# Every fourth weight residue of the routed experts is computed on GpSimd instead of VectorE

## The chip, the core and the metric

The kernel runs on one core of a Trainium2 chip. The metric is the device time of one execution in microseconds (us): 2703.51 us is the median of three runs (2703.31 to 2705.68). The engines are called as in the profile: PE (matmuls; PEld is its loading of weights), ACT (ScalarE), DVE (VectorE), POOL (GpSimd) and SP, whose queue issues the loads.

## The reference, cut to what matters

The network is a stack of three blocks on 256 tokens of width 1024. Its last stage before the final norm is a mixture of 8 experts, each a gated MLP of inner width 3584, and the two best experts of each token count:

```
logits = (xt @ w_router).astype(jnp.float32)
top_v, top_i = lax.top_k(logits, TOP_K)          # TOP_K = 2 of 8 experts
gates = jax.nn.softmax(top_v, axis=-1)
comb = jnp.sum(jax.nn.one_hot(top_i, N_EXPERTS) * gates[..., None], axis=1)
for e in range(N_EXPERTS):
    y = y + comb[:, e:e+1] * swiglu(xt, wg[e], wu[e], wd[e])   # (silu(x@wg) * (x@wu)) @ wd
```

All of it is in 32-bit floats. The kernel computes a product of two such matrices from rounded parts: each operand is split into a high part (rounded to the type that the profile calls fp32r) and a low part, the rest, and the products high x high, high x low and low x high are added up.

## The kernel before, in words

The weights of the experts come as pieces of 128 x 2048 numbers (1 MB). An expert has 7 groups (`NG`), and a group needs 6 pieces: 2 of the gate matrix, 2 of the up matrix and 2 of the down matrix. So there are 8 x 7 = 56 groups and 336 pieces. Five experts have room for 128 tokens and are called big here; three have room for 64 and are called small (`CAPS`). In the order in which they run, they are big, big, small, big, big, small, big, small.

A piece goes through four steps. SP issues its load into one of 13 buffers (4 of `raw`, 6 of `raw2`, 3 of `raw3`; the profile calls all of them raw). Then `load_e` hands its two halves of 128 x 1024, called half-blocks here, to `conv_w` (line 465). There ACT writes the high part, whi (line 470), and DVE subtracts it from the raw half-block and writes the low part, wlo (line 471). There are 4 buffers of whi and 4 of wlo (`W_BUFS`), so the conversion of a half-block starts when PE is done with the one four places before it. PE then multiplies with both parts: in `up` the gate product eg and the up product eu, in `down` or `down_small` the sum eacc. A big expert has 6 matmuls of 512 columns for a half-block (two with whi, one with wlo, twice), a small one has 4.

Beside the subtractions, DVE has two other operations in each group: eal (line 486) and ea (2019) in a big expert, eas (2038) and eax (486) in a small one. ACT has the matching copies and activations, es (2014) and ea (2018) among them.

Each engine runs its instructions in the order of its own queue, and waits with all that stands behind when the one at the front waits. A scheduler writes these orders out when the program is built. POOL has 72 memsets of small borders in the stages before the experts (lines 833 and 1205) and four at the start, and nothing in the experts.

Of the kernel before, what the change touches and what calls it, by code (L numbers as in the profile page):

```python
# [251 lines left out]
def hybrid_stack_kernel(ctx: ExitStack, tc: tile.TileContext, A, out, voff, coff, stages=STAGES):  # L252
    nc = tc.nc
    pe, act, dve, pool = nc.tensor, nc.scalar, nc.vector, nc.gpsimd
# [11 lines left out]
    turns = {n: [0, [("work", c[0]), ("attn", c[1])]] for n, c in (("t1", N_T1), ("t2", N_T2))}  # L266
# [25 lines left out]
    def raw_tile():  # L292
        i = raws["n"] % sum(n for _, n in raws["slots"])
        raws["n"] += 1
        for name, n in raws["slots"]:
            if i < n:
                if name == "ring":
                    return ring.tile([P, 2048], F32, tag="raw", name="raw", bufs=RAW_BUFS)
                return pools[name].tile([P, 2048], F32, tag=name, name=name, bufs=n)
            i -= n  # L300
# [35 lines left out]
    def f32v(ap):  # L336
        return ap.bitcast(F32)
# [101 lines left out]
    def load(name, i):  # L439
        if (name, i) in ahead:  # L440
            return ahead.pop((name, i))
        raw = raw_tile()
        nc.sync.dma_start(raw, A[name][i])
        return [conv_w(raw[:, j * 1024 : (j + 1) * 1024]) for j in range(2)]

    def prefetch(name, i, half=None, steps=1, between=None):
        if half is not None:
            if not half:
                ahead[name, i] = []
                ahead["raw"] = ring.tile([P, 2048], F32, tag="raw", name="raw", bufs=RAW_BUFS)  # L450
            raw = ahead["raw"][:, half * 1024 : half * 1024 + 1024]
            for j in range(steps):
                cs = slice(j * 1024 // steps, (j + 1) * 1024 // steps)
                nc.sync.dma_start(raw[:, cs], A[name][i][:, half * 1024 + cs.start : half * 1024 + cs.stop])
                if between and not j:
                    between()
            ahead[name, i].append(conv_w(raw, steps))
        elif (name, i) not in ahead:
            ahead[name, i] = load(name, i)
# [2 lines left out]
        prefetch(name, 2 * w)  # L462
        prefetch(name, 2 * w + 1)

    def conv_w(raw, n=1):
        hi = ring.tile([P, 1024], F32R, tag="whi", name="whi", bufs=W_BUFS)
        lo = ring.tile([P, 1024], F32R, tag="wlo", name="wlo", bufs=W_BUFS)
        for i in range(n):
            cs = slice(i * 1024 // n, (i + 1) * 1024 // n)
            act.copy(hi[:, cs], raw[:, cs])  # L470
            dve.tensor_sub(lo[:, cs], raw[:, cs], f32v(hi[:, cs]))  # L471
        return hi, lo

    def load_last(name, i):

        raw = raw_tile()
        r = []
        for j in range(2):
            cs = slice(j * 1024, j * 1024 + 1024)
            nc.sync.dma_start(raw[:, cs], A[name][i][:, cs])  # L480
            r.append(conv_w(raw[:, cs], 1 + j))
        return r
# [1430 lines left out]
    def moe_round(rnd, hth, htl, sel0, sel, comb, rest=None):  # L1913
        regs = {}

        def fetch(raw, src, e, i, cs=slice(0, 2048)):
            if e not in regs:
                regs[e] = None
                if e:
                    regs[e] = nc.values_load(  # L1920
                        route["idx"][0:1, e : e + 1], engines=[mybir.EngineType.SP], min_val=0, max_val=NE - 1
                    )
            if e:
                w = A[src][bass.ds(regs[e], 1), i : i + 1, :, cs].rearrange("a b p n -> (a b p) n")
            else:
                w = A[src][0, i][:, cs]
            nc.sync.dma_start(raw[:, cs], w)

        def load_e(src, e, i):
            raw = raw_tile()  # L1930
            fetch(raw, src, e, i)
            return [conv_w(raw[:, j * 1024 : (j + 1) * 1024]) for j in range(2)]

        def load_e_last(src, e, i):

# [59 lines left out]
        def up(x, g, mid):  # L1995
            e, gx, big = x[0], x[1], x[4]
            po = [wv("eg"), wv("eu")]
            po = [a.rearrange("p a b -> p (a b)") for a in po]
            s = []
            for i, src in enumerate(("moe_g", "moe_u")):  # L2000
                if i and mid:
                    mid()
                for c in range(2):
                    wt = load_e(src, e, 2 * g + c)
                    for k4 in range(4):
                        k = 4 * c + k4
                        whi, wlo = wt[k4 // 2]
                        cs = slice((k4 % 2) * 512, (k4 % 2 + 1) * 512)
                        for a in gx:
                            mm(po[i], a[:, k, :], whi[:, cs], k == 0 and a is gx[0], False)  # L2010
                        mm(po[i], gx[0][:, k, :], wlo[:, cs], False, k == KD - 1)
                if not big:
                    s.append(t2("es", (P, 512)))
                    act.copy(s[i], po[i])
            if not big:
                return s
            a = t2("ea", (P, 512))
            act.activation(a, po[0], AF.Silu)
            dve.tensor_mul(a, a, po[1])
            return a  # L2020
# [22 lines left out]
        def down(x, g, a, acc):  # L2043
            e = x[0]
            ah, al = a
            for c in range(2):
                wt = load_e("moe_d", e, 2 * g + c)
                for j in range(2):
                    f = slice((2 * c + j) * P, (2 * c + j + 1) * P)
                    whi, wlo = wt[j]  # L2050
                    for n in range(2):
                        cs = slice(n * 512, (n + 1) * 512)
                        first = g == 0 and c == 0 and j == 0
                        mm(acc[n], ah[:, f], whi[:, cs], first, False)
                        mm(acc[n], al[:, f], whi[:, cs], False, False)
                        mm(acc[n], ah[:, f], wlo[:, cs], False, g == NG - 1 and c == 1 and j == 1)

        def down_small(x, g, a, acc):

            e = x[0]  # L2060
            for c in range(2):
                end = e == NE - 1 and g == NG - 1 and c == 1
                wt = (load_e_last if end else load_e)("moe_d", e, 2 * g + c)
                for j in range(2):
                    whi, wlo = wt[j]
                    for n in range(2):
                        cs = slice(n * 512, (n + 1) * 512)
                        mm(acc[n], a[:, 2 * c + j, :], whi[:, cs], g == 0 and c == 0 and j == 0, False)
                        mm(acc[n], a[:, 2 * c + j, :], wlo[:, cs], False, g == NG - 1 and c == 1 and j == 1)
# [130 lines left out]
```

## Time and profile before

| | us |
|---|---|
| median of three runs | 2703.51 |
| the profiled execution, its time | 2704.3 |
| its span, first to last instruction | 2702.4 |
| DVE busy | 2189.1 |
| PE busy | 2630.7 |
| ACT busy | 1733.5 |
| POOL busy | 7.7 |

Busy times of the engines lie beside each other, so they don't add up to the span. The experts take the stretch from about 1722 to 2686 us. A matmul's end is modelled in such a profile, so a PE that is shown as busy may wait a little; its waits are read from the weight loads (PEld).

### The profile page before, as it was taken

The page shows a single profiled execution, that of the slowest core. Times are in us where ns is not written, and L with a number is a line of the kernel's source. Part 1 is how long each engine was busy: PE and PEld are TensorE (multiplying, and loading weights), DVE is VectorE, ACT ScalarE, POOL GpSimd, SP SyncE. Part 2 cuts the span into 40 slices and gives each one's busy share as a digit, 9 for nine tenths or more (in the row PEclk, how much of TensorE's full clock was granted, in tenths as well). Part 3 has the DMA queues.
Part 4 walks back from the last instruction along what each step waited for, and adds up shares of the span by engine and source line. Part 5 has one row for each costly group of instructions (what it writes and reads, how often), then busy time and mean ns, then how long its engine had stood idle before and what let it go on. Part 6 is the DMA issues. An engine that isn't in the chain of part 4 may idle for free. (4 is left out here: it accounts for less than half of the span.)

```text
span 2702.4 us, 44795 instructions
## 1 busy us (share of the span) xinstructions
PE 2630.7 (97%) x17220; PEld 2319.6 (86%) x17220; DVE 2189.1 (81%) x3385; ACT 1733.5 (64%) x2605; POOL 7.7 (0%) x76
## 2 busy tenths in 40 slices
PE   8999999999989999999999999999999999999997
PEld 8789999998989988888999999888876778767875
DVE  8787587789768776667885569789999888999898
ACT  6665565565656555455654446577788777787787
POOL 0000000000000000000000000000000000000000
PEclk9999999999999999999999999999999999999999
DMA  7145345533535543343655555799999999999993
GB/s 265 63 158 200 134 153 192 179 110 107 175 109 184 188 145 125 126 156 102 250 189 188 187 178 184 259 340 355 364 373 393 351 347 340 359 408 369 341 377 154
DMA packets 87262, 620.07 MB, mean 229 GB/s; under 512 B 9936, under 2 KB 10064, under 8 KB 12800
## 3 DMA queue, kind: packets, MB, share of 16 engines
q1 hardware_dynamic: 86608, 616.57, 62.3%
q8 instruction: 137, 2.24, 0.3%
q14 instruction: 85, 0.70, 0.1%
q10 hardware_dynamic: 432, 0.56, 0.1%
HBM read 616.04 MB, written 1.05 MB: 228 GB/s over the span
## 5 line engine op out<-in xcount | busy, mean ns | idle before, releaser
L471 DVE TENSOR_TENSOR wlo<-raw,whi 128x1024 fp32r<-128x1024 f32 (+1 forms) x1164 | 1387.7, 1218 | 324.6 <-ACT whi L470 318.7
L470 ACT CAST whi<-raw 128x1024 fp32r<-128x1024 f32 (+1 forms) x1164 | 1189.8, 1048 | 550.7 <-PE wv L334 290.4
L334 PE MATMUL wv<-hh,whi 128*128 128x256 f32 x2400 | 679.2, 284 | 14.2 <-ACT hh L669 13.0
L334 PE MATMUL wv<-hl,whi 128*128 128x256 f32 x2400 | 678.2, 283 | 0.1
L334 PE MATMUL wv<-hh,wlo 128*128 128x256 f32 x2400 | 674.9, 283 | 2.1 <-DVE wlo L471 1.8
L334 PEld LDWEIGHTS wv<-hh,whi 128*128 128x128 f32 x2400 | 456.5, 191 | 17.6 <-ACT hh L669 13.8
L334 PEld LDWEIGHTS wv<-hh,wlo 128*128 128x128 f32 x2400 | 455.4, 190 | 4.6 <-DVE wlo L471 3.7
L334 PEld LDWEIGHTS wv<-hl,whi 128*128 128x128 f32 x2400 | 456.8, 190 | 1.9 <-DVE hl L670 0.7
L334 PE MATMUL eu<-whi,gx 128*128 128x512 f32 x728 | 245.7, 400 | 0.0
L334 PE MATMUL eg<-whi,gx 128*128 128x512 f32 x728 | 245.0, 398 | 0.0
L334 PE MATMUL eg<-wlo,gx 128*128 128x512 f32 x448 | 184.8, 412 | 10.2 <-DVE wlo L471 9.9
L334 PE MATMUL eu<-wlo,gx 128*128 128x512 f32 x448 | 185.0, 413 | 5.0 <-DVE wlo L471 4.2
L334 PEld LDWEIGHTS eg<-whi,gx 128*128 128x128 f32 x728 | 137.0, 190 | 29.6 <-ACT whi L470 0.6
L334 PE MATMUL acc<-fl,whi 128*128 128x256 f32 x576 | 161.6, 281 | 0.0
L334 PE MATMUL acc<-fh,whi 128*128 128x256 f32 x576 | 161.4, 281 | 0.1
L334 PE MATMUL acc<-fh,wlo 128*128 128x256 f32 x576 | 161.3, 280 | 0.0
L334 PEld LDWEIGHTS eu<-whi,gx 128*128 128x128 f32 x728 | 135.3, 188 | 27.2 <-ACT whi L470 0.9
L334 PEld LDWEIGHTS eg<-wlo,gx 128*128 128x128 f32 x448 | 84.5, 189 | 51.8 <-DVE wlo L471 34.5
L845 DVE SCALAR_TENSOR_TENSOR cv<-pad,vec,cv 128x256 f32<-128x256 f32 x288 | 124.7, 478 | 1.4 <-ACT cv L842 0.6
L334 PEld LDWEIGHTS eu<-wlo,gx 128*128 128x128 f32 x448 | 84.1, 188 | 40.2 <-DVE wlo L471 23.3
L334 PE MATMUL eacc<-whi,eah 128*128 128x512 f32 x280 | 110.5, 395 | 0.0
L334 PE MATMUL eacc<-whi,eal 128*128 128x512 f32 x280 | 110.5, 395 | 0.0
(564 smaller groups left out, 4177.9 us busy)
## 6 DMA issues: line engine op xcount, KB each, us to landing
raw<-moe_u SPq DMA_DIRECT2D x112, 1024.0 KB, 6.4
raw<-moe_g SPq DMA_DIRECT2D x112, 1024.0 KB, 6.5
raw<-moe_d SPq DMA_DIRECT2D x111, 1024.0 KB, 6.2
raw<-ffn_in SPq DMA_DIRECT2D x44, 1024.0 KB, 4.9
raw<-sw_in SPq DMA_DIRECT2D x28, 1024.0 KB, 4.9
raw<-ffn_out SPq DMA_DIRECT2D x22, 1024.0 KB, 4.9
raw<-hy_in SPq DMA_DIRECT2D x20, 1024.0 KB, 5.0
raw<-ssm_in SPq DMA_DIRECT2D x18, 1024.0 KB, 5.1
```

Of the source, the lines that this page charges most:

```text
L334: return pe.matmul(o, l, r, start=start, stop=stop, skip_group_check=True)
L470: act.copy(hi[:, cs], raw[:, cs])
L471: dve.tensor_sub(lo[:, cs], raw[:, cs], f32v(hi[:, cs]))
L845: dve.scalar_tensor_tensor(y, pad[:, j, 4 - s : 4 + T - s], taps[i], y, op0=OP.mult, op1=OP.add)
```

## The change

`conv_w` gets an argument for the engine that subtracts. `load_e`, which loads all pieces of the experts but the very last, counts its calls, and in every odd call the second of the two half-blocks has its subtraction issued on POOL. That is one half-block in four. ACT's high parts, the buffers, the loads and the arithmetic stay.

```diff
-    def conv_w(raw, n=1):
+    def conv_w(raw, n=1, eng=None):
         hi = ring.tile([P, 1024], F32R, tag="whi", name="whi", bufs=W_BUFS)
         lo = ring.tile([P, 1024], F32R, tag="wlo", name="wlo", bufs=W_BUFS)
         for i in range(n):
             cs = slice(i * 1024 // n, (i + 1) * 1024 // n)
             act.copy(hi[:, cs], raw[:, cs])
-            dve.tensor_sub(lo[:, cs], raw[:, cs], f32v(hi[:, cs]))
+            (eng or dve).tensor_sub(lo[:, cs], raw[:, cs], f32v(hi[:, cs]))
         return hi, lo
...
         def load_e(src, e, i):
             raw = raw_tile()
             fetch(raw, src, e, i)
-            return [conv_w(raw[:, j * 1024 : (j + 1) * 1024]) for j in range(2)]
+            turns["lo"] = turns.get("lo", 0) + 1
+            return [
+                conv_w(raw[:, j * 1024 : (j + 1) * 1024], eng=pool if j and turns["lo"] % 2 else None) for j in range(2)
+            ]
```

The first place is DVE's queue in a group of a big expert, before. Each raw buffer has two subtractions, one for each of its half-blocks (the numbers behind the names are the program's buffers).

```order
L471 TENSOR_TENSOR wlo_21117<-raw_21114,whi_21116 128x1024
L471 TENSOR_TENSOR wlo_21121<-raw_21114,whi_21120 128x1024
L471 TENSOR_TENSOR wlo_21139<-raw_21136,whi_21138 128x1024
L471 TENSOR_TENSOR wlo_21143<-raw_21136,whi_21142 128x1024
L486 TENSOR_TENSOR eal_21111<-ept_21105,eah_21110 128x512
L471 TENSOR_TENSOR wlo_21164<-raw_21161,whi_21163 128x1024
L471 TENSOR_TENSOR wlo_21168<-raw_21161,whi_21167 128x1024
L471 TENSOR_TENSOR wlo_21186<-raw3_21183,whi_21185 128x1024
```

The same stretch of DVE's queue after the change.

```order
L471 TENSOR_TENSOR wlo_21117<-raw_21114,whi_21116 128x1024
L471 TENSOR_TENSOR wlo_21139<-raw_21136,whi_21138 128x1024
L471 TENSOR_TENSOR wlo_21143<-raw_21136,whi_21142 128x1024
L486 TENSOR_TENSOR eal_21111<-ept_21105,eah_21110 128x512
L471 TENSOR_TENSOR wlo_21164<-raw_21161,whi_21163 128x1024
L471 TENSOR_TENSOR wlo_21186<-raw3_21183,whi_21185 128x1024
```

The second half of raw_21114 and that of raw_21161 are gone from it; raw_21136 between them keeps both, and the rest keeps its order.

The second place is POOL's queue at the end of its memsets and the start of the experts, after the change (before, the end of the program follows on the memsets).

```order
L833 MEMSET pad_19628 128x2x4
L833 MEMSET pad_19640 128x2x4
L471 ISA
L471 TENSOR_TENSOR wlo_20083<-raw3_20076,whi_20082 128x1024
L471 TENSOR_TENSOR wlo_20127<-raw3_20120,whi_20126 128x1024
L471 TENSOR_TENSOR wlo_20266<-raw2_20259,whi_20265 128x1024
L471 TENSOR_TENSOR wlo_20319<-raw2_20312,whi_20318 128x1024
```

The subtractions of POOL stand one behind another with nothing between them. Ahead of the first stands a single instruction that reloads POOL's library of operations.

## Rows read from the trace of the kernel before

**Rows 1.** Windows: a big group, a small group, all experts (stretch, length, busy times)

```profile
core 0: us, PE busy (x) PEld busy (x) DVE busy (x) ACT busy (x) POOL busy (x), PEclk, DMA share, GB/s
1835.02:1852.25 17.23, 17.23 (x77) 13.91 (x76) 15.71 (x15) 13.48 (x16) 0.00 (x0) 1.00 0.99 371
2416.92:2432.08 15.16, 14.61 (x65) 10.29 (x64) 14.47 (x16) 13.22 (x17) 0.00 (x0) 1.00 1.01 414
1722.00:2686.00 964.00, 944.60 (x4251) 735.26 (x4249) 880.16 (x913) 757.16 (x879) 0.00 (x0) 1.00 0.92 352
```

**Rows 2.** Waits in the experts, 1722 to 2686 us: total, times, longest

```profile
DVE wlo L471 <- ACT whi L470: 53.8, 156, 1.7
...
PEld eg L334 <- DVE wlo L471: 34.5, 64, 1.1
ACT whi L470 <- PE eg L334: 32.6, 79, 1.9
ACT whi L470 <- PE eacc L334: 28.0, 78, 0.8
PEld eu L334 <- DVE wlo L471: 23.3, 56, 1.1
```

**Rows 3.** Timeline of ACT: starts of two groups, big, then small

```profile
1835.02 0.58 ACT L2018 ACTIVATE ea<-eg 128x512 f32<-128x512 f32 x1
1852.25 0.60 ACT L2018 ACTIVATE ea<-eg 128x512 f32<-128x512 f32 x1
...
2416.92 0.59 ACT L2014 COPY es<-eg 128x512 f32<-128x512 f32 x1 [1.09 <-PE eg L334]
2432.08 0.59 ACT L2014 COPY es<-eg 128x512 f32<-128x512 f32 x1 [1.10 <-PE eg L334]
```

**Rows 4.** Groups of DVE in the experts (count, busy us, mean ns, idle before)

```profile
L471 DVE TENSOR_TENSOR wlo<-raw,whi 128x1024 fp32r<-128x1024 f32 x670 | 786.3, 1218 | 57.8 <-ACT whi L470 53.8
L486 DVE TENSOR_TENSOR eal<-ept,eah 128x512 fp32r<-128x512 f32 x35 | 24.0, 686 | 8.6 <-ACT eah L485 8.6
L2019 DVE TENSOR_TENSOR ea<-ea,eu 128x512 f32<-128x512 f32 x35 | 23.9, 683 | 8.3 <-PE eu L334 8.2
...
L486 DVE TENSOR_TENSOR eax<-eas,eax 128x256 fp32r<-128x256 f32 x21 | 8.8, 417 | 0.3
L2038 DVE TENSOR_TENSOR eas<-eas,ept 128x256 f32<-128x256 f32 x21 | 8.7, 413 | 0.0
```

**Rows 5.** Timeline: DVE in the small group; then DVE and ACT in a big one

```profile
2426.39 6.89 DVE L471 TENSOR_TENSOR wlo<-raw,whi 128x1024 fp32r<-128x1024 f32 x6
...
1849.14 1.22 DVE L471 TENSOR_TENSOR wlo<-raw,whi 128x1024 fp32r<-128x1024 f32 x1 [0.17 <-ACT whi L470]
1850.54 1.22 DVE L471 TENSOR_TENSOR wlo<-raw,whi 128x1024 fp32r<-128x1024 f32 x1 [0.17 <-ACT whi L470]
...
1849.46 1.05 ACT L470 CAST whi<-raw 128x1024 fp32r<-128x1024 f32 x1 [0.35 <-PE eg L334]
```

**Rows 6.** Groups of POOL, whole program, with their shapes

```profile
L833 POOL MEMSET pad<- 128x8 f32 x64 | 6.5, 104 | 1228.9 <-DVE cv L845 1026.5 <-ACT cv L1156 89.1 <-ACT whi L470 55.3
L1205 POOL MEMSET dwp<- 128x30 f32 x8 | 1.0, 124 | 124.4 <-DVE cyd L1227 91.5 <-DVE cv L845 27.2 <-ACT cv L1156 5.7
```

**Rows 7.** POOL's memsets of pad: shortest, median, longest ns; first and last start

```profile
L833 POOL MEMSET pad<- x64: 104/104/107, 0.7 to 1361.1; 128x8 f32 x64
```

**Rows 8.** Timeline of DVE: the experts' first subtraction

```profile
1716.25 1.22 DVE L471 TENSOR_TENSOR wlo<-raw,whi 128x1024 fp32r<-128x1024 f32 x1
```

**Rows 9.** Waits of SP's queue in the experts: its longest

```profile
SPq L1927 <- DVE wlo L471: 630.2, 270, 6.4
```

## The prediction

> **What bounds the kernel now.** The chain that ended last covers only the final norm, so I read the experts by stretches: first the busy time of each engine over all experts and over one group of each kind, then who waits for whom, then the timeline inside a group.
>
> The experts take 964 us; PE is busy for 944.6 of them, DVE for 880.2, POOL for none [rows 1]. A big and a small group differ. A big group repeats every 17.23 us [rows 3], and PE is busy in all of it while DVE has 15.71 [rows 1]: PE is the bound. The timeline agrees: DVE's subtraction waits 0.17 us for ACT each time, and ACT waits 0.35 us for PE to give back a buffer [rows 5]. A small group repeats every 15.16 us [rows 3]; PE loses a part of it, and DVE is busy for 14.47 [rows 1]: there DVE is the bound, and its six subtractions stand without a gap [rows 5]. PE's weight loads wait for the low parts for 34.5 + 23.3 = 57.8 us in eg and eu [rows 2]. No wait for a load of raw data is among the longest, and SP waits 630.2 us for DVE to give buffers back [rows 9], so the loads run ahead.
>
> **What the change removes.** `load_e` is called 335 times, so 168 subtractions leave DVE: three of the twelve in a group. Back to back, six take 6.89 us and one alone 1.22, so one more costs (6.89 - 1.22) / 5 = 1.134 us [rows 5]. DVE is relieved of 3 x 1.134 = 3.4 us per group. In a big group this buys nothing of itself, since PE is full. In a small group DVE's need falls from 14.5 to 11.1 us, and the next engine is ACT with 13.22 us [rows 1].
>
> **What it adds: 168 subtractions on POOL.** The trace has none there, so I bound one. Below stands DVE's own, 1.22 us [rows 4]. Above, POOL's memsets: 30 columns take 124 ns, 8 take 104 [rows 6], so a column costs 0.91 ns and one stream of 1024 columns 0.93 us, with about 0.10 to start. A subtraction has two streams in and one out. If only the two inputs take turns, it takes 0.10 + 1.86 = 1.96 us; if all three do, 2.89. I take 1.96, which has the output written alongside as DVE does it.
>
> **Whether DVE goes on meanwhile.** That decides more than POOL's own time. DVE's subtraction has both inputs in SBUF, and its 1.134 us for 1024 columns is one column of each input every 1.1 ns: DVE fetches two streams at once, all the time. eas, with one input in PSUM, takes 413 ns for its 256 columns, and eax, with both in SBUF, takes 417 [rows 4], so the second stream costs DVE nothing today. POOL's two streams come on top of that. The two ends are that they run side by side, and that DVE's next subtraction stands still until POOL's is done. The memsets can't tell, as they read nothing. I take the second end for the forecast, because DVE's use of its second stream is nearly unbroken in both kinds of group, and count a handing over before and one after at the 0.17 us by which DVE follows ACT [rows 5]: 1.96 + 0.34 = 2.30 us in which no subtraction of DVE runs.
>
> The Trainium skill speaks to this. Its page "SBUF — State Buffer", section "Who interferes with whom", says that a VectorE instruction with two SBUF inputs and a GpSimd instruction that reads SBUF fetch through one shared port, and that the second to start is blocked until the first ends. No run here shows it yet. By it POOL's help would cost DVE more than it takes over. Its page "GPSIMD Engine Reference", section "3.1 Elementwise — side-by-side cycle accounting", gives 4497 ns for an addition of 2048 columns, so my estimate from that figure is 2.25 us for 1024; with the handing over that is 2.59, and the sum below would be +118 us instead of +72.
>
> **The sum, if they take turns.** A group then needs 3 x (2.30 + 3 x 1.134) = 17.1 us of turns. DVE's other two operations, eal and ea or eas and eax, may run while POOL holds DVE's subtractions up (then they add nothing) or not (then they add all).
> - Small group: 17.1 to 17.1 + 0.83 (413 + 417 ns [rows 4]) against 15.16: +1.95 to +2.78. Half way, 2.36, times 21 groups: +50 us.
> - Big group: 17.1 to 17.1 + 1.37 (686 + 683 ns [rows 4]) against PE's 17.23: 0 to +1.24. Half way, 0.62, times 35: +22 us.
>
> Together +72 us on the profiled 2704.3, so 2776; the median of the runs is 0.8 us lower, which changes nothing here. With POOL at 1.22 us, turns need 14.9 us a group, the big groups lose nothing and the small ones 0.13 us each: +3 us. With 2.89 us they need 19.9: +5.15 x 21 and +3.35 x 35, +225 us.
>
> **What I count at nothing.** PE's wait for POOL's low part: all of PE's queue stands behind it. In a big group a buffer given back by PE is needed again three half-blocks of 1.40 us later (the starts 1849.14 and 1850.54 [rows 5]) and its low part two matmuls after that; ACT takes 1.05 us of these 4.2 and two handings over 0.34, so 2.8 us are left for POOL, more than 2.30 and less than 2.89. In a small group three half-blocks of 15.16 / 12 leave 2.4 us: just enough. If this cover goes, each 0.1 us costs up to 17 us over 168 half-blocks. SP waits for POOL before it loads into every second buffer, about 1 us later than now; 13 buffers hide it. POOL's library is reloaded after its last memset at 1361.1 us [rows 7], and its first subtraction is due only at about 1716 [rows 8].
>
> **The rivals.**
> 1. *Side by side: faster.* If DVE isn't held up, the small groups shrink towards ACT's 13.22 us plus its waits of 1.1 us for PE at the group's start [rows 3], 14.3 us; against it the loads already move 414 GB/s there [rows 1], more than over the experts' mean of 352, and only the 13 buffers let the groups run ahead of them. 0.6 to 0.9 us times 21: -13 to -18 us; the big groups stay. About 2689. For it: ACT's casts and DVE's subtractions read the same buffers beside each other and keep their 1.05 and 1.22 us [rows 5].
> 2. *Turns column by column.* POOL's 1.86 us of reading is taken from DVE's second stream, no more. Small: 3 x (1.86 + 3.40) + 0.83 = 16.6 us, +1.45 x 21 = +30; big: 15.8 + 1.37 = 17.15, under PE's 17.23. About 2734. For it: big groups have 1.5 us of room in DVE [rows 1]. Against: DVE must be able to go on with every column that POOL leaves.
> 3. *POOL is slow.* Its three streams take turns: 2.89 us, +225 us, 2929. It decides from the point where POOL plus handing over passes the 2.4 and 2.8 us of cover; then PE waits for POOL's half-block itself. For it: POOL's cost of 0.91 ns for a column is for writing a constant, the least work there is.
>
> **How the numbers follow.** Turns by instruction (2776): 0.48. Side by side (2689): 0.22, of which 0.04 for so little that it isn't seen. Column by column (2734): 0.14, of which 0.03 within 0.2%. POOL slow (towards 2929): 0.16. 0.2% is 5.4 us, about what a measurement of this kernel can tell. So faster 0.18, same 0.07, slower 0.75. The forecast's own range is 2745 (1.95 x 21 = +41, nothing in the big groups) to 2806 (2.78 x 21 + 1.24 x 35 = +102). For 8 in 10 I take 2686 to 2870: the fast rival is in, and of the slow one the part up to a POOL of some 2.6 us.
>
> **What would show it.** POOL's rows give its subtraction: near 2.0 us, or 2.3 with waits in it. On DVE 502 subtractions of the experts' 670 [rows 4] remain; if they take turns, those that meet POOL last or wait longer, so that the mean rises above 1218 ns, by up to 2.30 / 3 us; if that mean stays at 1218, rival 1 holds. The small group goes to 17.1 us or more, the big one to between 17.2 and 18.5. If the weight loads' waits for POOL's wlo pass some tens of us, the cover was too thin. The forecast is wrong if small groups get shorter than 15.16 us, or big ones longer than 18.5.

## The result and the profile after

| | before | after |
|---|---|---|
| median of four runs, us | 2703.41 | 2838.76 |
| lowest and highest | 2702.10, 2705.68 | 2836.65, 2840.89 |
| span of the profiled execution | 2702.4 | 2835.5 |
| PE busy | 2630.7 | 2672.2 |
| DVE busy | 2189.1 | 2186.0 |
| POOL busy | 7.7 | 465.1 |
| mean granted clock of PE | 0.991 | 0.98 |

The change makes the kernel slower: the ratio is 1.0504, with a 95% interval of 1.0491 to 1.0516, or 135 us. DVE has 168 subtractions fewer and is as busy as before.

The windows of the kernel after answer to [rows 1]: a late big group, three small groups of like content, and all experts. The columns are those of [rows 1].

```profile
2227.08:2246.20 19.12, 18.01 (x77) 13.47 (x76) 14.27 (x11) 12.76 (x15) 8.73 (x4) 1.00 0.89 331
2443.43:2462.92 19.49, 15.85 (x65) 11.72 (x64) 14.77 (x12) 13.51 (x17) 7.63 (x4) 0.91 0.90 324
2484.76:2505.45 20.69, 17.04 (x65) 13.14 (x65) 14.85 (x12) 13.50 (x17) 8.36 (x4) 0.84 0.90 328
2505.45:2523.03 17.58, 14.72 (x65) 10.10 (x63) 13.45 (x11) 13.31 (x16) 7.72 (x4) 1.00 0.91 332
...
1722.00:2819.00 1097.00, 986.42 (x4248) 753.19 (x4247) 877.01 (x744) 762.54 (x879) 454.97 (x167) 0.97 0.84 309
```

The big group took 17.23 us before and PE filled it; here it takes 19.12 and PE has 18.01. The small group took 15.16 us; here it takes 17.6, 19.5 or 20.7, and the length goes with the granted clock, the third number from the end (1.00, 0.91, 0.84). Over all experts the clock was 1.00 and is 0.97.

The groups of DVE in the experts answer to [rows 4].

```profile
L471 DVE TENSOR_TENSOR wlo<-raw,whi 128x1024 fp32r<-128x1024 f32 x502 | 765.2, 1565 | 129.2 <-ACT whi L470 128.2
L486 DVE TENSOR_TENSOR eal<-ept,eah 128x512 fp32r<-128x512 f32 x35 | 23.9, 684 | 24.4 <-ACT eah L485 24.4
L2022 DVE TENSOR_TENSOR ea<-ea,eu 128x512 f32<-128x512 f32 x35 | 23.9, 682 | 23.9 <-PE eu L334 23.9
...
L486 DVE TENSOR_TENSOR eax<-eas,eax 128x256 fp32r<-128x256 f32 x21 | 16.9, 806 | 8.4 <-ACT eax L485 8.4
...
L1954 DVE TENSOR_SCALAR pm<-direct,selp 128x128 fp32r<-128x128 f32 x14 | 9.9, 724 | 0.0
```

A subtraction takes 1565 ns where it took 1218, and eax, with both inputs in SBUF, 806 where it took 417. eal and ea, each with one input in PSUM, keep their 684 and 682 ns. DVE's idle time before the subtractions rises too, from 57.8 to 129.2 us.

POOL's subtractions in the same experts (columns as in [rows 4]), and then the spread of DVE's: shortest, median and longest ns, first and last start.

```profile
L471 POOL TENSOR_TENSOR wlo<-raw,whi 128x1024 fp32r<-128x1024 f32 x168 | 457.4, 2722 | 996.4 <-ACT whi L470 956.1 <-PE eacc L334 9.2 <-PE eu L334 8.0
```

```profile
L471 POOL TENSOR_TENSOR wlo<-raw,whi x168: 2372/2584/3452, 1718.3 to 2813.5; 128x1024 fp32r<-128x1024 f32 x168
L471 DVE TENSOR_TENSOR wlo<-raw,whi x996: 678/1221/3423, 4.8 to 2817.6; 128x1024 fp32r<-128x1024 f32 x198, 128x512 fp32r<-128x512 f32 x2
```

The shortest on POOL is 2.37 us and the longest 3.45, which is 1.08 more, about one subtraction of DVE. DVE's longest is 3.42 us: its own 1.1 behind one of POOL's. The timeline of POOL and of DVE shows the two kinds of meeting.

```profile
1900.37 2.58 POOL L471 TENSOR_TENSOR wlo<-raw,whi 128x1024 fp32r<-128x1024 f32 x1 [3.63 <-ACT whi L470]
1905.96 3.20 POOL L471 TENSOR_TENSOR wlo<-raw,whi 128x1024 fp32r<-128x1024 f32 x1 [3.01 <-ACT whi L470]
```

```profile
1901.67 2.37 DVE L471 TENSOR_TENSOR wlo<-raw,whi 128x1024 fp32r<-128x1024 f32 x1 [0.98 <-ACT whi L470]
1903.95 0.67 DVE L2022 TENSOR_TENSOR ea<-ea,eu 128x512 f32<-128x512 f32 x1
1904.55 2.35 DVE L471 TENSOR_TENSOR wlo<-raw,whi 128x1024 fp32r<-128x1024 f32 x2
```

POOL's first ends at 1902.95. DVE's subtraction was begun at 1901.67 and ends at 1904.04, 1.09 us after POOL's end: it did its whole work then. POOL's second is begun at 1905.96, in the middle of two of DVE, which end at 1906.90; POOL ends at 1909.16, that is 2.26 us later. So whichever starts second stands still until the first is done. The rest of the trace agrees: 118 subtractions of DVE were begun beside one of POOL's and ended 1.08 to 1.19 us after it, and 141 of POOL's were begun beside one of DVE's and ended at least 2.22 us after it.

The waits in the experts answer to [rows 2] (total us, times, longest).

```profile
POOL wlo L471 <- ACT whi L470: 600.1, 155, 8.5
DVE wlo L471 <- ACT whi L470: 128.2, 123, 4.2
PEld eu L334 <- DVE wlo L471: 59.5, 36, 2.8
...
ACT eah L485 <- PE ept L2028: 49.6, 18, 3.7
...
PE eu L334 <- DVE wlo L471: 45.0, 24, 2.3
PEld eg L334 <- POOL wlo L471: 39.0, 37, 1.7
PEld eg L334 <- DVE wlo L471: 38.3, 63, 2.1
...
PEld eacc L334 <- POOL wlo L471: 21.8, 27, 1.7
```

In eg and eu the weight loads waited 57.8 us for low parts; now it is 97.8 us for DVE's alone, with waits up to 2.8 us where the longest was 1.1, and POOL's come on top. Matmuls of PE wait over 2 us in 17 places of the experts, each time for a subtraction of DVE that had met one of POOL's and so took 3.06 to 3.40 us.

Last, PE in a small group, first its timeline and then windows of 1 us (columns as in [rows 1]).

```profile
2443.23 0.39 PE L334 MATMUL eu<-whi,gx 128*128 128x512 f32 x1
2445.73 0.50 PE L334 MATMUL eu<-wlo,gx 128*128 128x512 f32 x1 [2.11 <-DVE wlo L471]
2446.07 0.39 PE L334 MATMUL eu<-whi,gx 128*128 128x512 f32 x1
...
2447.20 0.63 PE L334 MATMUL eu<-whi,gx 128*128 128x512 f32 x1
```

```profile
2443.00:2444.00 1.00, 0.62 (x3) 0.18 (x1) 1.00 (x1) 0.57 (x2) 1.00 (x1) 1.00 1.04 442
2444.00:2445.00 1.00, 0.00 (x0) 0.00 (x0) 1.00 (x1) 1.00 (x3) 0.59 (x1) 1.00 1.00 410
...
2446.00:2447.00 1.00, 1.00 (x5) 0.82 (x5) 1.00 (x2) 0.71 (x2) 0.00 (x0) 0.87 1.35 410
2447.00:2448.00 1.00, 1.00 (x3) 0.78 (x3) 1.00 (x2) 0.63 (x2) 0.00 (x0) 0.50 0.67 213
```

PE waits 2.11 us for DVE's low part, starts again at a clock of 1.00 (2.4 GHz), and about a microsecond later the clock goes to 0.50 (1.2 GHz): a matmul then takes 0.63 us instead of 0.39. Such a drop begins near 13 of the 17 waits above 2 us (at most 1.2 us from their end); others stand near shorter waits or near none. In the experts the clock stands at 0.50 for 68 us in all. Before, no group of a small expert had a clock below 1.00.

### The profile page after: what moved, and what is told of

Read it like the earlier page. It is cut to its first block, busy times and chain, and to the rows that moved or that the text cites. A ratio compares the mean times of both kernels' runs of the same rounds, so it can differ in the third digit from the quotient of the medians.

```text
span 2835.5 us, 44851 instructions
## 1 busy us (share of the span) xinstructions
PE 2672.2 (94%) x17220; PEld 2336.7 (82%) x17220; DVE 2186.0 (77%) x3217; ACT 1738.6 (61%) x2605; POOL 465.1 (16%) x244
## 5 line engine op out<-in xcount | busy, mean ns | idle before, releaser
L471 DVE TENSOR_TENSOR wlo<-raw,whi 128x1024 fp32r<-128x1024 f32 (+1 forms) x996 | 1365.6, 1393 | 395.7 <-ACT whi L470 393.0
L471 POOL TENSOR_TENSOR wlo<-raw,whi 128x1024 fp32r<-128x1024 f32 x168 | 457.4, 2722 | 996.4 <-ACT whi L470 956.1
L334 PE MATMUL eu<-whi,gx 128*128 128x512 f32 x728 | 255.5, 413 | 0.0
L334 PE MATMUL eu<-wlo,gx 128*128 128x512 f32 x448 | 193.5, 432 | 47.4 <-DVE wlo L471 45.0
L334 PE MATMUL eg<-wlo,gx 128*128 128x512 f32 x448 | 191.4, 427 | 39.0 <-POOL wlo L471 23.6
L833 POOL MEMSET pad<- 128x8 f32 x64 | 6.5, 105 | 1229.3 <-DVE cv L845 1008.5
L334 PEld LDWEIGHTS eu<-whi,gx 128*128 128x128 f32 x728 | 141.4, 197 | 29.5 <-ACT whi L470 0.2
```

The costliest lines, as they stand in the source:

```text
L334: return pe.matmul(o, l, r, start=start, stop=stop, skip_group_check=True)
L471: (eng or dve).tensor_sub(lo[:, cs], raw[:, cs], f32v(hi[:, cs]))
L833: pool.memset(p[:, :, 0:4], 0.0)
```

## The experiments

Each ratio is to the kernel before, timed in the same rounds (2702 to 2705 us). Line numbers of an experiment are a few higher where its edit adds lines.

**1 and 2. More buffers for the converted half-blocks.** Six instead of four of whi and wlo in the experts, two raw buffers fewer to make room; in the kernel after (w6_pool) and, as a control, in the kernel before (w6_dve).

```diff
-MORE_RAW = (6, 3)
+MORE_RAW = (6, 1)
+W_MORE = 2
...
+        pools["w2"] = ctx.enter_context(tc.tile_pool(name="w2", bufs=W_MORE))
...
+        if wi % (W_BUFS + W_MORE) < W_BUFS or wi < 0:
             hi = ring.tile([P, 1024], F32R, tag="whi", name="whi", bufs=W_BUFS)
             lo = ring.tile([P, 1024], F32R, tag="wlo", name="wlo", bufs=W_BUFS)
+        else:
+            hi = pools["w2"].tile([P, 1024], F32R, tag="whi2", name="whi2", bufs=W_MORE)
+            lo = pools["w2"].tile([P, 1024], F32R, tag="wlo2", name="wlo2", bufs=W_MORE)
```

> The changed kernel with 6 instead of 4 buffers each of whi and wlo in the experts, paid for with two of the 13 raw buffers. Theory A (turns at the port, and 4 buffers too few to hide them): the turns alone cost about 3 x (2.37 + 3 x 1.134) = 17.3 us a group, some +81 us over the same buffers without POOL, and the rest of the +135 us was PE waiting behind the ring of 4; so 2770 to 2795 us, and PE's weight loads wait for wlo less than half of the 176 us. Theory B (the turns themselves are dearer than that, buffers don't matter): 2825 us or more, waits as before.

> The control for the run above: the kernel before, with 6 buffers each of whi and wlo and 11 of raw. Both theories: near the kernel before, 2690 to 2706 us; its PE waits 66 us for wlo, of which the part in the small experts is DVE's speed and stays.

Measured: 2842.98 us (1.0517, 1.0499 to 1.0534) with POOL, and 2706.67 us (1.0006, 0.9997 to 1.0016) in the control. In the first two experts the big groups are back at 17.23 us, but the later big experts are 4 to 11 us longer than without the buffers, and the small ones between 3 us shorter and 2 us longer. The expected gain didn't come, and the time is theory B's. PE's waits for DVE's low part in eu are even longer:

```profile
PEld eu L336 <- DVE wlo L478: 71.3, 42, 2.8
```

Too few buffers explain two experts and not the whole. The queues' order is another than in the kernel after.

**3. POOL only writes.** It sets the low parts of its half-blocks to zero, so that these low parts are left out of the products.

```diff
-            (eng or dve).tensor_sub(lo[:, cs], raw[:, cs], f32v(hi[:, cs]))
+            if eng is None:
+                dve.tensor_sub(lo[:, cs], raw[:, cs], f32v(hi[:, cs]))
+            else:
+                eng.memset(f32v(lo[:, cs]), 0.0)
```

> In the changed kernel POOL writes a constant into its low parts instead of the subtraction (those low parts of the weights are left out), so it reads nothing from SBUF. Theory A (POOL's reading holds up DVE's subtractions): DVE's mean falls from 1565 to about 1220 ns and the time is 2680 to 2705 us, which is also what the relief of DVE is worth where nothing is held up. Theory C (any use of SBUF by POOL holds DVE up): DVE's mean stays above 1350 ns and the time above 2730 us.

Measured: 2702.11 us (0.9991, 0.9981 to 1.0000). The groups of DVE and of POOL:

```profile
L472 DVE TENSOR_TENSOR wlo<-raw,whi 128x1024 fp32r<-128x1024 f32 x500 | 593.2, 1221 | 174.0 <-ACT whi L470 173.3
```

```profile
L474 POOL MEMSET wlo<- 128x1024 f32 x167 | 159.3, 954 | 819.0 <-PE eg L334 313.9 <-PE eu L334 256.0 <-PE eacc L334 249.1
```

POOL's writing holds DVE up not at all (1221 ns). And with DVE relieved of a quarter at almost no price, the kernel gains nothing that can be told from no change: what DVE saves turns into waiting for ACT (174.0 us, before 57.8). The even small groups shrink to 14.7 us, but in the later big experts a group takes longer, though no turns are taken, as two starts of a group on ACT show:

```profile
2154.25 0.60 ACT L2024 ACTIVATE ea<-eg 128x512 f32<-128x512 f32 x1 [1.21 <-PE eg L334]
2172.31 0.60 ACT L2024 ACTIVATE ea<-eg 128x512 f32<-128x512 f32 x1 [1.93 <-PE eg L334]
```

That is 18.06 us where 17.23 stood [rows 3], with 77 matmuls in both. In it ACT waits 3.3 us at eah for PE's transposes (about 1.9 before), the casts behind come late, and PE waits 1.0 us for DVE's low part at eg. The likely cause is the order that the scheduler writes for the changed kernel: ACT and DVE have the same instructions in the same order here as in the kernel after, and so does PE but for four matmuls in one place. Beyond the stretch of DVE's queue shown ahead of the prediction, that order differs from the one before in many places, in ACT's queue too. So this run is the kernel after with its order and without its turns, and in all that order, with DVE relieved, costs nothing: what the later big groups lose, the small ones give back.

**4. POOL's subtraction in two pieces** of 512 columns.

```diff
+                for u in (slice(0, 512), slice(512, 1024)):
+                    eng.tensor_sub(lo[:, u], raw[:, u], f32v(hi[:, u]))
```

> The changed kernel with POOL's subtraction issued as two of 512 columns. Theory A with turns taken by instruction: DVE gets in between the two, so none of its subtractions lasts longer than about 2.5 us (now up to 3.42), and the time falls a little, 2800 to 2835 us. If the turns go by column, nothing but POOL's extra start is seen: 2838 to 2850 us, and DVE's longest stays.

Measured: 2794.31 us (1.0334, 1.0317 to 1.0352), a third of the loss gone. The spread of DVE's subtractions, and the window of a small group:

```profile
L472 DVE TENSOR_TENSOR wlo<-raw,whi x996: 680/1224/2369, 4.9 to 2773.6; 128x1024 fp32r<-128x1024 f32 x198, 128x512 fp32r<-128x512 f32 x2
```

```profile
2739.14:2757.19 18.05, 14.89 (x65) 10.20 (x64) 14.51 (x11) 13.32 (x17) 10.51 (x7) 1.00 0.12 44
```

DVE's longest falls from 3.42 to 2.37 us: it is held by one piece and not by two. So the turns are by instruction. The order is that of the kernel after (PE's again but for four matmuls). The clock of the small groups stays at 1.00, and they take about 18.06 us, which is longer than the best of the kernel after and shorter than its others.

**5. No POOL: DVE does the subtraction of those half-blocks twice.** DVE spends one turn more on each of them, and shares nothing.

```diff
+                for u in range(2):
+                    dve.tensor_sub(lo[:, cs], raw[:, cs], f32v(hi[:, cs]))
```

> No POOL at all: the kernel before, in which DVE does the subtraction of the half-blocks in question twice over. That takes 2 x 1.134 = 2.27 us of DVE for them, nearly what POOL's 2.37 us take from it. Theory A (all that POOL does is to make DVE unavailable for the length of its turn): 2795 to 2835 us, from 15 x 1.134 us and DVE's other two operations in each group (17.8 and 18.4 us against 15.16 and 17.23) upwards. Theory D (it is POOL's own lateness, or its queue, that costs): 2770 us or less.

Measured: 2831.75 us (1.0474, 1.0457 to 1.0492). The size is nearly that of the kernel after, the picture is another: DVE has hardly any idle time before its subtractions. The rows are of the stretch from 1722 to 2700 us, which ends before the last experts do; L472 has the single subtractions, L475 both of each pair.

```profile
L472 DVE TENSOR_TENSOR wlo<-raw,whi 128x1024 fp32r<-128x1024 f32 x447 | 535.4, 1216 | 7.8 <-ACT whi L470 7.4 <-PE eu L334 0.4
L475 DVE TENSOR_TENSOR wlo<-raw,whi 128x1024 fp32r<-128x1024 f32 x298 | 362.7, 1217 | 18.2 <-ACT whi L470 18.0
```

The time is theory A's: taking DVE away for some 2.3 us per half-block is enough for a loss of this size, though the order is another than in the kernel after.

**6. Four pieces** of 256 columns, the edit as in experiment 4.

```diff
+                for u in (slice(i * 256, i * 256 + 256) for i in range(4)):
+                    eng.tensor_sub(lo[:, u], raw[:, u], f32v(hi[:, u]))
```

> The changed kernel with POOL's subtraction issued as four of 256 columns. If the length of one turn is what hurts, beside the time that all turns take, it falls below the 2794 us of two pieces: 2765 to 2790 us, and no subtraction of DVE is held up by more than some 0.7 us at a time. If POOL's starts now eat the gain: 2795 to 2820 us, and POOL's summed time for a half-block passes 3.5 us.

Measured: 2919.13 us (1.0789, 1.0770 to 1.0808): both expected times fell. A piece takes 0.72 us undisturbed and 1.07 on average, since each may find DVE in its way; a half-block's four sum up to 4.3 us, which does pass the 3.5 named. So the whole low part comes later than in one piece, and PE waits for it (in the kernel after, 21.8 and 39.0 us):

```profile
PEld eacc L334 <- POOL wlo L475: 97.9, 59, 3.0
...
PEld eg L334 <- POOL wlo L475: 79.2, 47, 3.0
```

**7. POOL reads one input.** It copies whi into its low parts, so these hold wrong numbers.

```diff
+                eng.tensor_copy(lo[:, cs], f32v(hi[:, cs]))
```

> In the changed kernel POOL copies whi into its low parts instead of subtracting (those low parts are wrong numbers), so it reads one tensor and writes one. If the length of the turn goes with the streams that POOL reads: some 1.2 us each, turns of 3 x (1.2 + 3.4) = 13.8 us a group, which is less than DVE's 14.5 now; 2700 to 2725 us, DVE's mean 1250 to 1400 ns. If any reading by POOL is as dear as the subtraction: above 2800 us.

Measured: 2706.84 us (1.0013, 1.0003 to 1.0022).

```profile
L474 POOL CAST wlo<-whi 128x1024 fp32r<-128x1024 f32 x168 | 213.6, 1271 | 1109.4 <-ACT whi L470 1086.3 <-PE eg L334 11.3 <-PE eu L334 8.0
```

```profile
L472 DVE TENSOR_TENSOR wlo<-raw,whi x996: 684/1224/2058, 5.6 to 2685.5; 128x1024 fp32r<-128x1024 f32 x198, 128x512 fp32r<-128x512 f32 x2
```

It takes 1.27 us on average, and DVE's longest is 2.06 us, so they still meet, yet the mean of DVE's subtraction is only 1.23 us. The 32 subtractions of DVE that were begun beside a copy ended 1.07 to 1.21 us after it, so a copy holds DVE up as well; in the kernel after there are 118 such, and each stands still for longer. Turns that are shorter than what DVE was relieved of (undisturbed, a copy takes 1.04 us and a subtraction of DVE 1.13) cost almost nothing. ACT, DVE and PE have exactly the order of the kernel after here. So the 132 us between these two kernels come from POOL's subtraction, and not from the order.

**8. One half-block in eight.**

```diff
-                conv_w(raw[:, j * 1024 : (j + 1) * 1024], eng=pool if j and turns["lo"] % 2 else None) for j in range(2)
+                conv_w(raw[:, j * 1024 : (j + 1) * 1024], eng=pool if j and turns["lo"] % 4 == 1 else None) for j in range(2)
```

> The change with half the dose: one half-block in eight on POOL, 84 in all. If every meeting of the two engines costs the same 0.8 us (135 / 168), half of it: 2765 to 2778 us. If the room that DVE has left takes up the first ones and only the rest costs, less than half: 2715 to 2755 us.

Measured: 2758.05 us (1.0200, 1.0183 to 1.0217). Half as many cost 55 us, 0.41 of the 135; the result lies between the two theories and decides nothing.

**9 and 10. Another half-block of the four**: the first of each pair of loads (`not j and turns["lo"] % 2`), and the last (`j and turns["lo"] % 2 == 0`).

> The changed kernel with the same number of half-blocks on POOL, but the first instead of the second of the four half-blocks of each product. Theory A (only the sum of the turns counts): same time, 2825 to 2850 us. Theory E (a turn costs most where ACT next stands in its queue for PE's finished product, as at es and ea, since the casts behind it then come late for both DVE and POOL; so a late low part counts more the nearer it is to a product's end): earlier is better, 2790 to 2825 us.

> The changed kernel with the same number of half-blocks on POOL, but the last instead of the second of the four of each product. Theory A: same time, 2825 to 2850 us. Theory E: the low part that PE needs to finish the product is now POOL's, and all of its 2.4 to 3.4 us stand ahead of es or ea: 2855 us or more.

Measured: 2847.28 us (1.0539, 1.0522 to 1.0557) and 2870.51 us (1.0627, 1.0609 to 1.0645). Theory E is right on the last and wrong on the first, and theory A the other way round. The place, with the order that the scheduler writes for it, is worth some 30 us; no simple rule of the place holds.

**11 and 12. PE kept busy.** Small experts only: the first product with a high part is done six times, each time starting the sum anew; ahead of PE's longest wait (busy_at_the_wait, at the up matrix) or at the gate matrix (busy_elsewhere, with `not i` for `i`).

```diff
-                        for a in gx:
+                        for a in (list(gx[:1]) * 5 if i and not k and not big else []) + list(gx):
```

> The kernel after, with five matmuls more at one place of each small expert's group: the first product of the up matrix with its high part is done six times, each starting the sum anew, so that the result stays the same. It stands just ahead of the place where PE waits longest for a low part of DVE (2.1 us in most small groups), and where the trace of the kernel after then shows a granted clock of 0.50 for some 3 us. Small groups of that kernel with like content take 17.6 us where the clock stays at 1.00, 19.5 at 0.91 and 20.7 at 0.84. Theory C, that part of the loss is PE's clock, which falls after these waits: with some 1.2 us of matmuls in it the wait is near 0.9 us, the clock of small groups is at or above 0.97, groups come near 17.6 to 18.3 us, and the time is 2785 to 2815 us although PE has 105 matmuls more. Theory L, that the loop of ACT, DVE, POOL and PE sets the pace and the slow clock only fills PE's waits: 2830 to 2855 us, groups at their length, whatever the clock.

> The same five matmuls more per small group, but at the first product of the gate matrix, where PE waits little for DVE's low part (the longest such waits of PE stand at the up matrix). Theory C: the wait of 2.1 us at the up matrix and the slow stretch behind it stay, and the time is 2835 to 2865 us. Theory L: 2830 to 2865 us as well. If this kernel gains as much as the one with the matmuls at the wait, it isn't their place that counts, and the gain would be laid to the order that the scheduler writes.

Measured: 2822.53 us (1.0440, 1.0422 to 1.0457) and 2830.99 us (1.0479, 1.0461 to 1.0496). 105 matmuls more, and 16 and 8 us less than the kernel after. The first is above theory C's range and below theory L's; the second is below theory C's and just inside theory L's. Part of the gain may be the order, which the scheduler changes with the matmuls. Two neighbouring small groups of the second show the clock's price more cleanly, for their engines do the same work:

```profile
2754.11:2772.37 18.26, 15.30 (x70) 11.36 (x69) 14.78 (x12) 13.45 (x16) 7.99 (x4) 1.00 0.91 332
2772.37:2791.90 19.53, 16.75 (x70) 12.75 (x69) 14.80 (x12) 13.51 (x16) 7.93 (x4) 0.91 0.07 29
```

The same 70 matmuls take 1.45 us more and the group 1.27 more. In the first run, four of the last five small groups take 18.26 to 18.27 us or 20.74 with a clock of 1.00.

## Why the prediction was right, and where it was not

The direction and the turns hold; the sum gave +72 us and +135 were measured. The time lies in the wider range, 2686 to 2870 us, but above the forecast's own, 2745 to 2806. The room above 2806 was meant for a POOL of up to 2.6 us, and POOL takes 2.37: that the wider range holds is partly luck. By the steps of the prediction:

- **What the change removes:** right. 168 subtractions left DVE, worth 168 x 1.134 = 191 us; in experiment 3, without turns, DVE's busy time in them falls by 786.3 - 593.2 = 193. In a big group it bought nothing, as said.
- **POOL's own time:** too low. 1.96 us was taken; the shortest in the trace is 2.37 us, between the bound of two streams in turn (1.96) and that of three (2.89), so neither is shown. The 0.34 us of handing over isn't in the trace: DVE ends as little as 1.08 us after POOL, less than its 1.13. The two errors nearly cancel, and it is luck that 2.30 us came so close to the length of a turn. The Trainium skill's "GPSIMD Engine Reference", section "3.1 Elementwise — side-by-side cycle accounting", led to an estimate of 2.25 us: nearer.
- **Whether DVE goes on meanwhile:** it doesn't, shown by the timeline and by experiment 4. The 502 subtractions left to DVE were stretched by 502 x (1.565 - 1.218) = 174 us, 1.04 us for each of POOL's, and POOL's own by 457.4 - 168 x 2.37 = 59 us. "SBUF — State Buffer", section "Who interferes with whom", of the Trainium skill states that the second to start is blocked until the first ends, and the trace agrees: DVE did its whole work, 1.09 us, after POOL's end. Experiment 3 shows that POOL's writes don't count.
- **The small group:** the term was right where PE's clock stayed at 1.00. Forecast +1.95 to +2.78, taken 2.36; measured 17.6 against 15.16, so +2.4. But only 4 of the 18 whole small groups in the trace are that short, and one of these (17.48) took 13.90 before. The other like groups take 19.5 or 20.7 us.
- **The big group:** the halfway point failed. DVE's eal and ea were to be hidden half behind POOL's turns. From the first start of a big expert to that of the next, the five take 46 us more in all, 1.3 per group, where 0.62 was taken. With 2.37 us for POOL instead of 2.30, the upper end is 1.24 + 3 x 0.07 = 1.45, so the measured value is near the end at which these operations add all. But that these operations are the cause isn't shown: DVE stands 24.4 and 23.9 us before them, where 8.6 and 8.3 stood [rows 4], but in experiments 3 and 7, with the same order and next to no loss, it stands 36.5 and 17.2. Experiment 3 also has late big groups of 18.06 us with no turns at all, so up to 0.8 us of such a group comes with the order. Its five big experts are only 3 us longer than before in all, so some 43 of the 46 us come with the turns. Groups of 19.1 us also pass the 18.5 that the prediction named as a mark of failure: by its own sign, it was wrong on the big group.
- **What was counted at nothing:** this is the step that failed most. The weight loads waited 66 us for POOL's low parts, past the "some tens of us" that the prediction named as the sign of too thin a cover; the cover of 2.4 and 2.8 us was worked out from an even group. And a price was given only for POOL's half-block. In the trace it is DVE's low part that PE waits for longest (2.1 us at eu in most small groups), because that subtraction of DVE stood behind one of POOL's. With all waits for low parts, PE's weight loads stood 176 us, 110 of them for DVE's; before it was 67, all for DVE's. ACT's standing at eah (49.6 us) isn't the cause: experiment 7 has 46.9 without the loss.
- **PE's clock:** not in the prediction at all. Near most waits of some 2 us the granted clock drops to 0.50 for a few us, and the same matmuls take longer: PE is busy for 14.72 us in the small group at 1.00 and for 17.04 in that at 0.84.

Adding up what the trace has: 21 small groups at +2.4 are 50 us (forecast 50). The three small experts are 88 us longer in all (from their first group's start to the next expert's, the last one to the end of the program), so 38 us more come from longer waits and the clock. The five big experts are 46 us longer (forecast 22). That is 134 us, where the two profiled spans differ by 133; the experts start 1.4 us earlier after the change.

How the 38 us divide between the waits and the clock is only bounded. The clock stood at 0.50 for 68 us in the experts, so it took at most 34 us of PE's work. Of two like groups, one with the drop is 1.27 us longer in experiment 12, and 1.9 to 3.1 in the kernel after, where the waits differ too. Experiment 11 got back 16 us, but the order had changed as well. Experiment 4 has the order of the kernel after and no drop of the clock in the experts (0.992 on the mean) and still costs some 90 us, so the clock is not the main part. The order isn't it either: experiments 3 and 7 have that of the kernel after and take 2702 and 2707 us. What stays open is why the place of POOL's half-block is worth 30 us (experiments 9 and 10, each with an order of its own): no theory of mine foretold which place.

On the rivals: side by side fell, by the timeline. Its price of -13 to -18 us was wrong too: experiment 3 is that case nearly free of any hold, and it gave 0.9991. There the even small groups do shrink, by 0.5 us, and late big ones grow by 0.8. Column by column fell with the 1.09 us and with experiment 4, and a POOL of 2.89 us with the 2.37. What rival 3 said of the point at which PE waits for POOL came true at a POOL of 2.37 us: 66 us of such waits in the kernel after, and more in experiment 6, by pieces that arrive late.

No version beats the kernel before. Even a nearly free relief of DVE is worth nothing here, in the order that the scheduler writes for it, so there was nothing to win.

## What to carry to other kernels

Before moving work off a busy engine, run the version in which the work is simply gone from it: here that was worth nothing, and it takes one run to know. Where an engine's reads hold up the one that it should relieve, as POOL's did here, it takes whole turns, so its instruction has to be shorter than the work it takes over: a copy of 1.04 us all but broke even, and at 2.37 us against 1.13 the trade was lost from the start. A forecast that adds turns holds for the undisturbed group; what comes on top, here PE waiting 2 us for a low part and then running at half its clock, needs a term of its own.

## What the runs showed of the hardware

- POOL's times in us, the shortest of each: subtraction of two fp32 inputs 2.37 (1024 columns), 1.27 (512), 0.72 (256); a copy of 1024 columns 1.04; a memset of 1024 columns 0.95 on average.
- A tensor_scalar of DVE with 128 columns (pm) takes 724 ns on average where it took 278. Three of the 14 were begun beside a subtraction of POOL and took 2.3 to 2.4 us, so it is held up as well, not only operations with two tensors.
- In two pieces POOL's subtraction costs less (2794 us), in four more (2919) than in one (2839).
- After a wait of PE of 2.1 us, as near 13 of the 17 waits above 2 us, its granted clock stood at 0.50 for some 3 us, and a matmul of 512 columns took 0.63 us instead of 0.39, in a kernel whose experts ran at 1.00 throughout before.
